# A decoder block on one core: three small edits to its vector work, and a planner that chooses its order with margins and jitter

## The chip, the cores and the metric

One Trainium2 chip, one of its cores. Five engines take part, each with an instruction queue of its own: TensorE (PE: matrix products), VectorE (DVE), ScalarE (ACT), GpSimd (POOL) and SyncE (SP, which issues most of the transfers). The metric is the device time of one execution in microseconds (us), as the median of several runs; less is better.

## The reference

A decoder block on x of 1024 positions by 1024 channels, all in float32. Two mixers share the input projection, a dense gated feed-forward network (FFN) follows, and a final norm:

```python
cond = silu(c) @ ada_w + ada_b                 # shift1, scale1, gate1, shift2, scale2, gate2
h = rmsnorm(x, norm1_g) * (1 + scale1) + shift1
u, v, val, gate = split(h @ w_in + b_in)       # 512 channels each
# mixer A: spatial gating, 8 heads of 64, causal in chunks of 128 positions
v = layernorm(gelu(v), a_ln_g, a_ln_b)
y_a = gelu(u) * (einsum('hts,bcshd->bcthd', tril(w_s), v) + b_s)
# mixer B: gated causal depthwise convolution of width 31, norm by 8 groups, swish
y_b = silu(groupnorm(conv(val * sigmoid(gate)) + conv_b))
x = x + gate1 * (concat(rmsnorm(y_a), rmsnorm(y_b)) @ w_out)
h2 = rmsnorm(x, norm2_g) * (1 + scale2) + shift2
g_ff, up = split(h2 @ w_ffn_in)                # 2 x 2816 channels
x = x + gate2 * ((silu(g_ff) * up) @ w_ffn_out)
out = rmsnorm(x, norm_f_g) * (1 + scale_f) + shift_f
```

## The kernel before

Activations are held transposed, channels on the 128 partitions, and the 1024 positions in two halves of 512; most tiles are 128x512. A float32 product is made of three fp32r products of a high and a low part (`mm3`, L679 to L684, for the mixers; `product`, L1068 to L1074, for the FFN, with `split` at L1064 making the two parts). The FFN uses a seven-product scheme of Strassen's kind, whose PSUM banks appear as A, B and C. `ah` are products of the FFN's first tiles, made ahead while the mixers of the other half still run.

The places that the change touches:

- `v_proj` (L895): the gelu of v leaves PSUM through ScalarE into `vn[half][tch]`, four tiles of 128 positions by 512 channels for each half. Mean and variance go into `mv`, ScalarE takes the root `sd` (L917), DVE its reciprocal (L918), and DVE normalises each tile in place (L921): eight passes of 128x512 in all.
- `spatial` (L941): for each pair of heads, eight small products of 64 columns (L947) fill a PSUM bank `pm` from the four `vn` tiles. One DVE pass scales it and adds the bias into an SBUF tile `mx` (L951), another multiplies `ya`, the gelu of u, by it (L955). Eight of each in all.
- `finish_shift` and `finish_scale` (L646 to L652): DVE adds the bias to a few columns of `cond`, and forms `(1 + scale) * gain`. Each pass is 128 by 8 elements.
- `conv_pair` (L985): the 31 taps of the convolution, most of them on DVE (L1006, `cv`), some as an ACT product and a POOL sum (L1000, L1001).
- `rstd` (L710): sums of squares by narrow products of 32 columns (L727), root on ACT (L730), reciprocal on DVE (L731), spread back by a product of PE (L737).
- the conditioning itself: DVE forms part of the columns of `cond` (L636), POOL and ACT the rest (L633, L634).
- `norm` and `output` (L1370, L1380): the last norm, `rt_nf` on DVE at L1375, spread by PE at L1377, and the output tiles `of` on DVE (L1399), ACT and out by a transfer.

The order on each engine is not that of the code. `fix_order` (L499), called last, has all instructions with their dependences and PSUM slots, gives each a cost, and simulates: `forward` lays them out by rank, `backward` finds for each how long the rest after it takes, and that becomes the next rank. Four such orders are made (a first one and three more), the one that ends first by the simulation is kept, and each engine's row is fixed by dependences that need no semaphore.

Of the kernel before, what the change touches and what calls it, by code (L numbers as in the profile page):

```python
# [67 lines left out]
ENGINES = ("PE", "DVE", "Activation", "Pool", "SP")  # L68
SIGNAL = {"PE": 0.043, "DVE": 0.024, "Activation": 0.024, "Pool": 0.068, "SP": 0.05}
TABLES = ("Sqrt", "Silu", "Sigmoid", "Gelu")  # L70
TABLE_LOAD = 1.295
LOAD_WAIT, STORE_WAIT, LOAD_RATE, STORE_RATE = 2.05, 1.29, 350e3, 376e3
LOAD_GAP, STORE_GAP, TURN_GAP = 0.07, 0.24, 0.3
DMA_ISSUE = 0.44
DMA_AHEAD = 0.5
SHORT_ROWS = 1.15
CLOCK_WINDOW = 3.4133


class Step:  # L80
# [313 lines left out]
def forward(g, rank):  # L394

    import heapq
    count = len(g.steps)
    need, at = [len(s.before) for s in g.steps], [0.0] * count
    done, order = [0.0] * count, {e: [] for e in ENGINES}
    ready, waiting = ({e: [] for e in ENGINES} for _ in range(2))  # L400
    parked = {tag: [] for tag in g.order}
    slots, clock, table = Slots(g), Clock(True), None

    def arrive(n):
        tag, t = slots.blocked_on(g.steps[n])
        if tag is not None:
            parked[tag].append(n)
            return
        heapq.heappush(waiting[g.steps[n].engine], (max(at[n], t), n))

    def wake(tags):
        for tag in tags:
            again, parked[tag] = parked[tag], []
            for n in again:
                arrive(n)

    for s in g.steps:
        if not need[s.n]:
            arrive(s.n)
    for _ in range(count):  # L420
        t, e = pick(clock, ready, waiting)
        while waiting[e] and waiting[e][0][0] <= t + 1e-6:
            n = heapq.heappop(waiting[e])[1]
            heapq.heappush(ready[e], (rank[n], n))
        chosen = ready[e][0]
        if e == "Activation" and g.steps[chosen[1]].table not in (None, table):
            others = [x for x in ready[e] if g.steps[x[1]].table in (None, table)]
            if others and min(others)[0] < chosen[0] + TABLE_LOAD:
                chosen = min(others)
# [12 lines left out]
        for n in s.after:  # L442
            need[n] -= 1
            same = g.steps[n].engine == e and not s.dma
            if (s.n, n) in g.turns:
                at[n] = max(at[n], t + DMA_ISSUE)
            else:
                at[n] = max(at[n], (clock.free[e] if e == "PE" else end) if same else end + SIGNAL[e])
            if not need[n]:
                arrive(n)  # L450
    return order, done, slots.follows
# [44 lines left out]
    return tail  # L496


def fix_order(tc, edges, stacked, reusing, rounds=3):  # L499

    g = Graph(list(tc.nc.cur_bb.bb.instructions), edges, stacked, reusing)
    order, done, follows = forward(g, list(range(len(g.steps))))
    best = max(done), order
    for _ in range(rounds):
        tail = backward(g, [-t for t in done], follows)
        order, done, follows = forward(g, [-t for t in tail])
        best = min(best, (max(done), order), key=lambda b: b[0])
    for steps in best[1].values():
        for earlier, later in zip(steps, steps[1:]):
            tc.add_manual_dep(later.ins, earlier.ins.name,  # L510
                              mybir.DependencyInfo(mybir.DependencyClass.NoSync, mybir.DependencyReason.DATA),
                              reason="fix_order")
# [3 lines left out]
def block_kernel(ctx: ExitStack, tc: tile.TileContext, xT, c, ada, cols, vbias, bs, wsp,  # L516
                 wv, wu, wk, wvg, wo, wf, wfo, wfl, cst, out):
    nc = tc.nc
    V, A, G, PE = nc.vector, nc.scalar, nc.gpsimd, nc.tensor

    edges = []
# [7 lines left out]
    const = ctx.enter_context(tc.tile_pool(name="const", bufs=1))  # L529
# [5 lines left out]
    mid = stage.enter_context(tc.tile_pool(name="mid", bufs=1))  # L535
    front = stage.enter_context(tc.tile_pool(name="front", bufs=1))
# [21 lines left out]
    def tmp(name, dt=F32):  # L558
        return front.tile([P, H], dt, tag="tmp", name=name, bufs=N_TMP)
# [7 lines left out]
    colt = const.tile([P, NCOL], F32, name="colt")  # L567
# [10 lines left out]
    def col(name, i=0):  # L578
        o = _OFF[name] + i
        return colt[:, o:o + 1]  # L580
# [58 lines left out]
    def ccol(m, k, n=1):  # L639
        return cond[:, m * 8 + k:m * 8 + k + n]  # L640

    def bcol(m, k, n=1):
        o = _OFF["ada_b"] + m * 8 + k
        return colt[:, o:o + n]

    def finish_shift(m, k, n):  # L646
        V.tensor_tensor(ccol(m, k, n), ccol(m, k, n), bcol(m, k, n), op=ALU.add)

    def finish_scale(m, gname, k, n):
        o = _OFF[gname] + k  # L650
        V.tensor_tensor(ccol(m, k, n), ccol(m, k, n), bcol(m, k, n), op=ALU.add)
        V.scalar_tensor_tensor(ccol(m, k, n), ccol(m, k, n), 1.0, colt[:, o:o + n],  # L652
                               op0=ALU.add, op1=ALU.mult)


    def weights(src, name, lo_eng, tag="w", parts=1):
# [106 lines left out]
    bst = front.tile([P, 4, P], F32, name="bst")  # L763
# [81 lines left out]
    for k in range(KD):  # L845
        n = len(nc.cur_bb.bb.instructions)
# [13 lines left out]
        t = tmp(f"t_h1_0_{k}")  # L860
# [34 lines left out]
    def v_proj(half, between=None):  # L895
        mv = const.tile([P, 4, 2], F32, name=f"mv{half}")
        sd = const.tile([P, 4], F32, name=f"sd{half}")
        vn[half] = [front.tile([P, H], F32, tag="vn", name=f"vn{half}_{i}", bufs=4) for i in range(4)]
        if not vw:
            vw.extend(weights(wv[i], f"v_{i}", G) for i in range(4))  # L900
        for tch in range(4):
            bank = mm_bank(f"v{half}_{tch}")
            tok = slice(tch * P, (tch + 1) * P)
            for k in range(KD):
                hk = h1[half][k]
                mm3(bank, (hk[:, 0, tok], hk[:, 1, tok]), unit(vw[k // 2], k % 2, 512),
                    k == 0, False)
            PE.matmul(bank, vsel.broadcast_to([P, P]), vb, start=False, stop=True)
            dst = vn[half][tch]
            A.activation(dst, bank, AF.Gelu)  # L910
            st = front.tile([P, 6], F32, tag="bn", name=f"bn{half}_{tch}", bufs=4)
            V.bn_stats(st, dst)
            V.bn_aggr(mv[:, tch, :], st)
            step_background()
            if between is not None and tch == 1:
                between()
        A.activation(sd, mv[:, :, 1], AF.Sqrt, bias=epst[:, 0:1])  # L917
        V.reciprocal(sd, sd)  # L918
        for tch in range(4):
            dst = vn[half][tch]  # L920
            V.tensor_scalar(dst, dst, mv[:, tch, 0:1], sd[:, tch:tch + 1],  # L921
                            op0=ALU.subtract, op1=ALU.mult)

    ya = [None, None]

    def ya_part(half, j):
        return ya[half][j // 2][:, hs(j % 2)]
# [13 lines left out]
    def spatial(half, bank):  # L941
        for hp in range(4):
            pm = bank(f"pm{half}_{hp}")
            for tch in range(4):
                for e in range(2):
                    o = hp * P + e * 64
                    PE.matmul(pm[e * 64:(e + 1) * 64, tch * P:(tch + 1) * P],  # L947
                              vn[half][tch][:, o:o + 64],
                              wt[:, 2 * hp + e, :], start=True, stop=True)
            t = tmp(f"mx{half}_{hp}")  # L950
            V.scalar_tensor_tensor(  # L951
                t.rearrange("p (c t) -> p c t", c=4), pm.rearrange("p (c t) -> p c t", c=4),
                col("a_ln_g", hp), bst[:, hp:hp + 1, :].broadcast_to([P, 4, P]),
                op0=ALU.mult, op1=ALU.add)
            V.tensor_tensor(ya_part(half, hp), ya_part(half, hp), t, op=ALU.mult)  # L955

    def branch_out(half, srcs, gname, name, ssq_groups, add_eng, lo_eng):
        r = rstd(srcs, DA, name, ssq_groups, add_eng)
# [185 lines left out]
    ffn = ctx.enter_context(tc.tile_pool(name="ffn", bufs=1, reuse_waits="tile"))  # L1144
# [44 lines left out]
    for f in range(N_AHEAD, N_AHEAD + N_FILL):  # L1189
        t = ffn.tile([P, 2, H], F32, tag="m3", name=f"ahead_{f}", bufs=4)  # L1190
# [4 lines left out]
    for p in range(4):  # L1195
        b11, b21, b12, b22 = (ev(f"h2_{n}_{p}") for n in ("11", "21", "12", "22"))
        for kh, (t0, t1) in enumerate(((b11, b12), (b21, b22))):
            k = p + 4 * kh
# [59 lines left out]
    order = tile_order()  # L1258
# [236 lines left out]
    output(1)  # L1495
    output(2)

    fix_order(tc, edges, ("mid", "front"), "ffn", 3)


# [79 lines left out]
```

## Time and profile before

| | |
|---|---|
| median of 3 runs | 968.09 us (967.17 to 968.7) |
| the profiled execution's own time | 967.97 us |
| its span in the profile | 965.9 us |
| granted TensorE clock, mean | 0.995 |
| PE, PEld busy | 98%, 80% of the span |
| DVE, ACT, POOL busy | 90%, 49%, 42% |
| moved by transfers | 184 MB, 191 GB/s |

The span runs from the first to the last instruction; 2.07 us of the execution lie around it. PEld is TensorE loading weights, which runs beside its products. A busy PE is not by itself a PE at full rate: matmuls overlap, so the distance between the starts of two matmuls says more than the busy share. A group's row gives the line, the engine and operation, output from inputs, the count, busy us in all and mean ns of one, and then the idle time before and what ended it.

### The profile page before, as it was taken

The numbers are of one execution on the slowest core, as the hardware profiler recorded it, in microseconds if no ns is written. First come the engines' busy times: TensorE is split into PE (matmuls) and PEld (weight loads), VectorE is DVE, ScalarE is ACT, GpSimd is POOL, SyncE is SP. The second block draws the span as 40 slices with busy tenths as digits, with TensorE's granted clock in tenths as the row PEclk, the third lists the DMA queues.
The fourth block names the chain that finished last, engine by engine and source line by source line (L and its number), as shares of the span: only waits on it lengthen the run. The fifth ranks groups of instructions, "written<-read, shape, count | busy, mean of one in ns | idle before, by whom it ended". The sixth has DMA issues, their size and how long they took to land.

```text
span 965.9 us, 12960 instructions
## 1 busy us (share of the span) xinstructions
PE 950.5 (98%) x4521; PEld 769.6 (80%) x4521; DVE 871.7 (90%) x1236; ACT 474.0 (49%) x756; POOL 408.6 (42%) x241
## 2 busy tenths in 40 slices
PE   8999999999999999999999999999999999999996
PEld 4887777778777778788888888888888888888885
DVE  6999999999999763999999999999879999969956
ACT  5787477643474753564333333333337437227426
POOL 0089988836453413665444444455433100000132
PEclk9999999999999999999999999999999999999998
DMA  9882542343485444844677678867657857415104
GB/s 353 323 310 91 176 152 69 113 174 131 137 282 188 158 136 146 271 173 147 215 245 239 230 237 261 268 211 257 211 177 264 266 172 258 162 33 159 61 1 174
DMA packets 70498, 184.24 MB, mean 191 GB/s; under 512 B 7841, under 2 KB 8353, under 8 KB 70434
## 3 DMA queue, kind: packets, MB, share of 16 engines
q1 hardware_dynamic: 70434, 183.43, 56.5%
q8 instruction: 35, 0.57, 0.2%
q14 instruction: 29, 0.24, 0.1%
HBM read 142.24 MB, written 41.16 MB: 190 GB/s over the span
## 4 chain that ended last, share of the span: by engine, by line
PE 79%; DVE 15%; ACT 2%; DMA 2%; issue 1%; SPq 0%; ACTq 0%; DVEq 0%
PE B L1073 30%; PE C L1073 18%; PE ah L1073 10%; DVE cv L1006 5%; PE A L1073 3%; PE v L682 2%; PE v L684 2%; PE po L682 2%; PE po L684 2%; PE v L683 2%; PE po L683 2%; PE p L684 1%; PE p L683 1%; PE p L682 1%; DVE ada L636 1%
## 5 line engine op out<-in xcount | busy, mean ns | idle before, releaser
L1073 PE MATMUL B<-h,w_f 128*128 128x512 f32 x816 | 189.6, 389 | 0.1
L1073 PEld LDWEIGHTS B<-h,w_f 128*128 128x128 f32 x816 | 153.0, 188 | 32.5 <-ACT x L1291 0.8
L1006 DVE SCALAR_TENSOR_TENSOR cv<-ypad,colt,cv 128x512 f32<-128x512 f32 x216 | 147.0, 744 | 0.2
L1073 PE MATMUL B<-fa,w_d 128*128 128x512 f32 x528 | 124.8, 389 | 0.1
L1073 PE MATMUL C<-h,w_f 128*128 128x512 f32 x528 | 123.4, 389 | 0.0
L1073 PEld LDWEIGHTS B<-fa,w_d 128*128 128x128 f32 x528 | 98.8, 188 | 21.4 <-DVE x L1433 0.7
L1073 PEld LDWEIGHTS C<-h,w_f 128*128 128x128 f32 x528 | 99.1, 188 | 20.6
L1073 PE MATMUL ah<-h,wh_a 128*128 128x512 f32 x320 | 102.4, 396 | 0.3 <-ACT h L699 0.3
L1359 POOL TENSOR_TENSOR sq_nf<-sq_nf,sq_nf 128x512 f32<-128x512 f32 (+1 forms) x15 | 18.0, 1202 | 170.2 <-ACT sq_nf L1353 170.0
L666 POOL TENSOR_TENSOR wl_a<-raw_a,wh_a 128x1024 fp32r<-128x1024 f32 x20 | 49.8, 2488 | 78.2 <-ACT wh_a L665 78.2
L1065 ACT ACTIVATE w_d<-raw_d 128x512 fp32r<-128x512 f32 (+1 forms) x72 | 42.0, 593 | 80.9 <-PE B L1073 32.6
L1065 ACT ACTIVATE w_f<-raw_f 128x512 fp32r<-128x512 f32 x68 | 42.5, 629 | 75.9 <-PE B L1073 41.5
L1316 POOL TENSOR_TENSOR x<-x,up 128x512 f32<-128x512 f32 x20 | 33.2, 1659 | 105.6 <-ACT x L1315 105.6
L1066 DVE TENSOR_TENSOR w_f<-raw_f,w_f 128x512 fp32r<-128x512 f32 x68 | 70.2, 1039 | 2.6 <-ACT w_f L1065 2.5
L1073 PEld LDWEIGHTS ah<-h,wh_a 128*128 128x128 f32 x320 | 60.0, 188 | 15.7 <-ACT h L699 1.4
L1073 PE MATMUL C<-fa,w_d 128*128 128x512 f32 (+1 forms) x291 | 63.9, 370 | 0.0
L1073 PE MATMUL ah<-h,wl_a 128*128 128x512 f32 x160 | 62.5, 390 | 0.0
L1073 PEld LDWEIGHTS C<-fa,w_d 128*128 128x128 f32 x291 | 51.0, 188 | 9.2
L1066 DVE TENSOR_TENSOR fa<-a,fa 128x512 fp32r<-128x512 f32 x77 | 52.4, 720 | 0.4 <-ACT fa L1065 0.4
L1433 DVE SCALAR_TENSOR_TENSOR x<-B,cond,x 128x512 f32<-128x512 f32 x48 | 35.6, 745 | 18.2 <-PE B L1073 18.0
L1066 DVE TENSOR_TENSOR w_d<-raw_d,w_d 128x512 fp32r<-128x512 f32 (+1 forms) x72 | 49.1, 691 | 1.1 <-ACT w_d L1065 1.1
L1065 ACT ACTIVATE fa<-a 128x512 fp32r<-128x512 f32 x77 | 46.1, 625 | 7.1 <-DMA a<-acts 4.0
(265 smaller groups left out, 2111.2 us busy)
## 6 DMA issues: line engine op xcount, KB each, us to landing
acts<-x SPq DMA_DIRECT2D x77, 256.0 KB, 2.9
a<-acts SPq DMA_DIRECT2D x77, 256.0 KB, 4.0
raw_f<-wf SPq DMA_DIRECT2D x32, 512.0 KB, 4.0
ada<-ada SPq DMA_DIRECT2D x24, 512.0 KB, 3.5
x<-ada SPq DMA_DIRECT2D x24, 512.0 KB, 4.4
raw_a<-wf SPq DMA_DIRECT2D x20, 512.0 KB, 3.9
ahead<-ahead SPq DMA_DIRECT2D x40, 256.0 KB, 2.6
ypad<-ada SPq DMA_DIRECT2D x16, 512.0 KB, 5.7
```

Of the source, the lines that this page charges most:

```text
L636: V.scalar_tensor_tensor(raw, raw, 1.0, cact, op0=ALU.mult, op1=ALU.mult, accum_out=cond[:, j:j + 1])
L666: lo_eng.tensor_tensor(lo[:, cut], raw[:, cut], hi[:, cut].bitcast(F32), op=ALU.subtract)
L682: PE.matmul(acc, shi, mhi, start=start, stop=False)
L683: PE.matmul(acc, slo, mhi, start=False, stop=False)
L684: PE.matmul(acc, shi, mlo, start=False, stop=stop)
L1006: V.scalar_tensor_tensor(accs[j], src, wc, accs[j], op0=ALU.mult, op1=ALU.add)
L1065: A.activation(dst[:, 0, :], src, AF.Copy)
L1066: lo_eng.tensor_tensor(dst[:, 1, :], src, dst[:, 0, :].bitcast(F32), op=ALU.subtract)
L1073: last_mm = PE.matmul(bank[:, cols], s, m[:, cols], start=first and p == 0 and i == 0, stop=p == n - 1 and i == 2, skip_group_check=True)
L1316: G.tensor_tensor(g0, g0, up0, op=ALU.mult)
L1359: G.tensor_tensor(run, run, t, op=ALU.add)
L1433: V.scalar_tensor_tensor(x_tile(k, part), bank[:, cols], ccol(GATE2, k), x_tile(k, part), op0=ALU.mult, op1=ALU.add)
```

## The change

1. `spatial`: the scaled and biased result is written back to the PSUM bank `pm`, and the product with `ya` reads it there. The SBUF tile `mx` is gone.
2. `v_proj`: a DVE pass of 128x4 forms `nb = -mean * sd`; the eight normalisations become ScalarE activations with `sd` as scale and `nb` as bias.
3. `finish_shift`, `finish_scale`: from DVE to GpSimd; the scale takes three passes in place of two, through a tile `gained`.
4. `fix_order`: the costs of all instructions but PE's are stretched by 1, 1.5 or 2%, those of transfers by 5, 7.5 or 10%. For each of the three margins four ranked orders are made, and of the twelve the one is kept whose mean end is earliest over four replays with random lengthening.

```diff
-def fix_order(tc, edges, stacked, reusing, rounds=3):
+MARGINS = ((1.01, 1.05), (1.015, 1.075), (1.02, 1.1))
+JITTER = (0.008, 0.08)
+TRIALS = 4
+def replay(g, order):
+    ... # runs a given order through the same slots, clock and costs; returns when the last step ends
+@contextmanager
+def stretched(g, factor):
+    kept = [(s, s.issue, s.finish, s.port, s.dma and s.bytes) for s in g.steps if s.engine != "PE"]
+    for s, issue, finish, port, size in kept:
+        f = factor(s)
+        if s.dma:
+            s.bytes = size * f
+        else:
+            s.issue, s.finish, s.port = issue * f, finish * f, port * f
+    yield
...
+def jittered(g, order, seed):
+    rng = random.Random(seed)
+    with stretched(g, lambda s: 1 + abs(rng.gauss(0, JITTER[s.dma]))):
+        return replay(g, order)
+
+def fix_order(tc, edges, stacked, reusing, rounds=4):
     g = Graph(list(tc.nc.cur_bb.bb.instructions), edges, stacked, reusing)
-    order, done, follows = forward(g, list(range(len(g.steps))))
-    best = max(done), order
-    for _ in range(rounds):
-        tail = backward(g, [-t for t in done], follows)
-        order, done, follows = forward(g, [-t for t in tail])
-        best = min(best, (max(done), order), key=lambda b: b[0])
-    for steps in best[1].values():
+    orders = []
+    for margin in MARGINS:
+        with stretched(g, lambda s: margin[s.dma]):
+            order, done, follows = forward(g, list(range(len(g.steps))))
+            for _ in range(rounds):
+                tail = backward(g, [-t for t in done], follows)
+                order, done, follows = forward(g, [-t for t in tail])
+                orders.append(order)
+    times = [sum(jittered(g, order, seed) for seed in range(TRIALS)) for order in orders]
+    best = orders[times.index(min(times))]
+    for steps in best.values():
...
     def finish_shift(m, k, n):
-        V.tensor_tensor(ccol(m, k, n), ccol(m, k, n), bcol(m, k, n), op=ALU.add)
+        G.tensor_tensor(ccol(m, k, n), ccol(m, k, n), bcol(m, k, n), op=ALU.add)
     def finish_scale(m, gname, k, n):
         o = _OFF[gname] + k
-        V.tensor_tensor(ccol(m, k, n), ccol(m, k, n), bcol(m, k, n), op=ALU.add)
-        V.scalar_tensor_tensor(ccol(m, k, n), ccol(m, k, n), 1.0, colt[:, o:o + n],
-                               op0=ALU.add, op1=ALU.mult)
+        G.tensor_tensor(ccol(m, k, n), ccol(m, k, n), bcol(m, k, n), op=ALU.add)
+        gained = const.tile([P, n], F32, name=f"gained{m}")
+        G.tensor_tensor(gained, ccol(m, k, n), colt[:, o:o + n], op=ALU.mult)
+        G.tensor_tensor(ccol(m, k, n), gained, colt[:, o:o + n], op=ALU.add)
...
         V.reciprocal(sd, sd)
+        nb = const.tile([P, 4], F32, name=f"nb{half}")
+        V.scalar_tensor_tensor(nb, mv[:, :, 0], -1.0, sd, op0=ALU.mult, op1=ALU.mult)
         for tch in range(4):
             dst = vn[half][tch]
-            V.tensor_scalar(dst, dst, mv[:, tch, 0:1], sd[:, tch:tch + 1],
-                            op0=ALU.subtract, op1=ALU.mult)
+            A.activation(dst, dst, AF.Identity, bias=nb[:, tch:tch + 1], scale=sd[:, tch:tch + 1])
...
-            t = tmp(f"mx{half}_{hp}")
-            V.scalar_tensor_tensor(
-                t.rearrange("p (c t) -> p c t", c=4), pm.rearrange("p (c t) -> p c t", c=4),
-                col("a_ln_g", hp), bst[:, hp:hp + 1, :].broadcast_to([P, 4, P]),
-                op0=ALU.mult, op1=ALU.add)
-            V.tensor_tensor(ya_part(half, hp), ya_part(half, hp), t, op=ALU.mult)
+            chunks = pm.rearrange("p (c t) -> p c t", c=4)
+            V.scalar_tensor_tensor(chunks, chunks, col("a_ln_g", hp), bst[:, hp:hp + 1, :].broadcast_to([P, 4, P]),
+                                   op0=ALU.mult, op1=ALU.add)
+            V.tensor_tensor(ya_part(half, hp), ya_part(half, hp), pm, op=ALU.mult)
...
-    fix_order(tc, edges, ("mid", "front"), "ffn", 3)
+    fix_order(tc, edges, ("mid", "front"), "ffn")
```

The new planner gives every engine a new row. Lines of the changed kernel stand 66 or 67 further down (L947 becomes L1015, L1006 becomes L1072, L731 becomes L798, L1399 becomes L1465).

On TensorE, at the first products of the spatial mixer for half 0 (`pm0_0` is written `pm_0_1271`; `v` are the wide products of the projection of v for half 1). In the row before:

```order
L683 MATMUL v_1_1359<-wh_v_991,h_1_6_828 128x512
L947 MATMUL pm_0_1271<-wt,vn_0_958 64x128 x2
L947 MATMUL pm_0_1271<-wt,vn_1_959 64x128 x2
L947 MATMUL pm_0_1271<-wt,vn_2_960 64x128 x2
L947 MATMUL pm_0_1271<-wt,vn_3_961 64x128 x2
L947 MATMUL pm_1_1283<-wt,vn_0_958 64x128 x2
```

and in the row now:

```order
L749 MATMUL v_0_1323<-wh_v_991,h_1_6_828 128x512
L1015 MATMUL pm_0_1273<-wt,vn_0_958 64x128 x2
L750 MATMUL v_0_1323<-wh_v_991,h_1_6_828 128x512
L1015 MATMUL pm_0_1273<-wt,vn_1_959 64x128 x2
L751 MATMUL v_0_1323<-wl_v_992,h_1_6_828 128x512
L1015 MATMUL pm_0_1273<-wt,vn_2_960 64x128 x2
L1015 MATMUL pm_1_1284<-wt,vn_0_958 64x128
L1015 MATMUL pm_0_1273<-wt,vn_3_961 64x128 x2
```

They stand in the projection's first chunk (`v_0`) where they stood in its second (`v_1`), that is 26 wide products earlier, and single wide products now lie between them. In the whole row of TensorE the unbroken blocks of narrow products (32 or 64 columns) go from 24 to 28, counted without the very first block, which handles c; one of the four additional ones lies in the head, ahead of the first wide products. The two sums `gn` over the convolution's outputs in half 1 (L1026, `s` by `cstt`), of which there are two pairs, had six and three other products between the two of a pair; now the two stand next to each other, the first of the first pair eight rows later than before.

On VectorE, ahead of the reciprocal for the norm of the second half of x (`rt_n1_1`), taps of the convolution are `cv`, conditioning columns `ada`. In the row before:

```order
73 L636 TENSOR_SCALAR ada20_966,cond_107<-ada20_966,cact_99 128x1024
74 L1006 TENSOR_SCALAR cv0_0_1144<-ypad0_108,colt_74,cv0_0_1144 128x512
75 L1006 TENSOR_SCALAR cv0_1_1145<-ypad1_109,colt_74,cv0_1_1145 128x512
76 L1006 TENSOR_SCALAR cv0_0_1144<-ypad0_108,colt_74,cv0_0_1144 128x512
77 L1006 TENSOR_SCALAR cv0_1_1145<-ypad1_109,colt_74,cv0_1_1145 128x512
78 L731 RECIPROCAL rt_n1_1_783<-rt_n1_1_783 128x128
```

and in the row now:

```order
72 L702 TENSOR_SCALAR ada20_966,cond_107<-ada20_966,cact_99 128x1024
73 L1072 TENSOR_SCALAR cv0_1_1147<-ypad1_109,colt_74,cv0_1_1147 128x512
74 L798 RECIPROCAL rt_n1_1_783<-rt_n1_1_783 128x128
75 L1072 TENSOR_SCALAR cv0_0_1146<-ypad0_108,colt_74,cv0_0_1146 128x512
76 L1072 TENSOR_SCALAR cv0_1_1147<-ypad1_109,colt_74,cv0_1_1147 128x512
```

The reciprocal stands four instructions nearer to the front, one tap behind the same conditioning pass where four stood.

On VectorE at the end of the program (`of1` and `of2` are output tiles of the last two quarters of the positions, `rt_nf2` the last quarter's root). In the row before:

```order
1135 L1399 TENSOR_SCALAR of1_4_8307<-x1_2_81,cond_107,ssq_nf1_8199 128x256 x2
1136 L1375 RECIPROCAL rt_nf2_8290<-rt_nf2_8290 128x2
1137 L1399 TENSOR_SCALAR of1_6_8313<-x1_3_82,cond_107,ssq_nf1_8199 128x256 x2
1138 L1399 TENSOR_SCALAR of2_0_8319<-x1_0_79,cond_107,ssq_nf2_8200 128x256 x2
```

and in the row now:

```order
1111 L1465 TENSOR_SCALAR of1_4_8307<-x1_2_81,cond_107,ssq_nf1_8199 128x256 x2
1112 L1465 TENSOR_SCALAR of1_6_8313<-x1_3_82,cond_107,ssq_nf1_8199 128x256
1113 L1441 RECIPROCAL rt_nf2_8290<-rt_nf2_8290 128x2
1114 L1465 TENSOR_SCALAR of1_6_8313<-x1_3_82,cond_107,ssq_nf1_8199 128x256
1115 L1465 TENSOR_SCALAR of2_0_8319<-x1_0_79,cond_107,ssq_nf2_8200 128x256 x2
```

The last reciprocal stands one pass of 128x256 later.

More of the change, by code (lines that the diff above doesn't have):

```diff
@@ L496, in backward @@
     return tail
-def fix_order(tc, edges, stacked, reusing, rounds=3):
-    g = Graph(list(tc.nc.cur_bb.bb.instructions), edges, stacked, reusing)
-    order, done, follows = forward(g, list(range(len(g.steps))))
-    best = max(done), order
-    for _ in range(rounds):
-        tail = backward(g, [-t for t in done], follows)
-        order, done, follows = forward(g, [-t for t in tail])
-        best = min(best, (max(done), order), key=lambda b: b[0])
-    for steps in best[1].values():
+def replay(g, order):
+    place, done, at = dict.fromkeys(ENGINES, 0), {}, [0.0] * len(g.steps)
+    need = [len(s.before) for s in g.steps]
+    slots, clock, table = Slots(g), Clock(True), None
+    for _ in range(len(g.steps)):
+        best = None
+        for e in ENGINES:
+            if place[e] == len(order[e]) or need[order[e][place[e]].n]:
+                continue
+            s = order[e][place[e]]
+            tag, t = slots.blocked_on(s)
+            t = max(t, at[s.n], clock.free[e])
+            if tag is None and (best is None or t < best[0]):
+                best = t, s
+        t, s = best
+        slots.take(s)
+        if s.table not in (None, table):
+            table, t = s.table, t + TABLE_LOAD
+        begin, end = clock.run(s, t)
+        done[s.n] = end
+        if slots.release(s, end + SIGNAL[s.engine]):
+            slots.hand_over()
+        for n in s.after:
+            need[n] -= 1
+            if (s.n, n) in g.turns:
+                at[n] = max(at[n], t + DMA_ISSUE)
+            elif g.steps[n].engine == s.engine and not s.dma:
+                at[n] = max(at[n], clock.free["PE"] if s.engine == "PE" else end)
+            else:
+                at[n] = max(at[n], end + SIGNAL[s.engine])
+        place[s.engine] += 1
+    return max(done.values())
@@ new lines, in stretched @@
+@contextmanager
[5 more added lines that the diff above has]
+            s.bytes = size * f
+        else:
+            s.issue, s.finish, s.port = issue * f, finish * f, port * f
+    yield
+    for s, s.issue, s.finish, s.port, size in kept:
+        if s.dma:
+            s.bytes = size
+def jittered(g, order, seed):
+    import random
+    rng = random.Random(seed)
+    with stretched(g, lambda s: 1 + abs(rng.gauss(0, JITTER[s.dma]))):
+        return replay(g, order)
```

## The prediction

> **What bounds the kernel now.** I read the page first: the busy shares and the chain that ended last.
>
> ```profile
> PE 950.5 (98%) x4521; PEld 769.6 (80%) x4521; DVE 871.7 (90%) x1236; ACT 474.0 (49%) x756; POOL 408.6 (42%) x241
> ...
> PE 79%; DVE 15%; ACT 2%; DMA 2%; issue 1%; SPq 0%; ACTq 0%; DVEq 0%
> ```
>
> TensorE is busy 98% and carries 79% of the chain, but VectorE has 90%. So I looked at the stages, in the windows of equal length (columns: stretch, length, busy us of PE, PEld, DVE, ACT and POOL with counts, then PE clock, DMA share, GB/s).
>
> ```profile
> 160.00:180.00 20.00, 20.00 (x149) 15.11 (x149) 19.54 (x28) 14.05 (x21) 15.55 (x8) 1.00 0.50 158
> 460.00:480.00 20.00, 20.00 (x90) 16.57 (x89) 19.79 (x25) 6.55 (x11) 8.86 (x6) 1.00 0.62 210
> ```
>
> In both, VectorE is nearly full (19.54 and 19.79 of 20 us), and PE doesn't wait: 20.00 of 20. VectorE runs full beside it, with buffers between. VectorE time removed is worth something only where PE waits for it. Those places are in the list of waits, engine PE (us in all, times, longest).
>
> ```profile
> PE ssq_nf L1377 <- DVE rt_nf L1375: 1.5, 1, 1.5
> ...
> PE ssq_n L737 <- DVE rt_n L731: 1.0, 1, 1.0
> PE ssq_n L825 <- ACT sq_n L823: 0.5, 1, 0.5
> PE ah L1073 <- ACT h L699: 0.3, 1, 0.3
> PE gn L1026 <- DVE s L1049: 0.2, 1, 0.2
> ```
>
> L825 is in the head, as others left out here are, which hang on the first transfers and have none of the edited steps. L1377 is the tail. What remains of note between is 1.0, 0.3 and 0.2 us. So the kernel is bound by TensorE, and there is little to win: the three mid-program waits show 1.5 us idle. A wait costs more than its idle time, as the next matmul starts late too; doubled, 3.0 us is my bound for them.
>
> **The edits on VectorE (1, 2 and 3).** Their prices, from the groups by shape:
>
> ```profile
> L921 DVE TENSOR_SCALAR vn<-vn,mv,sd 128x512 f32<-128x512 f32 x8 | 10.7, 1373 | 0.0
> L955 DVE TENSOR_TENSOR ya<-ya,mx 128x512 f32<-128x512 f32 x8 | 9.6, 1222 | 0.0
> L1318 DVE TENSOR_TENSOR u<-C,u 128x512 f32<-128x512 f32 x22 | 15.0, 682 | 2.2 <-PE C L1073 2.2
> L647 DVE TENSOR_TENSOR cond<-cond,colt 128x8 f32<-128x8 f32 x4 | 3.7, 954 | 0.0
> ```
>
> L921 goes: 10.7 us. L955 gets one input from PSUM; the same operation with a PSUM input is L1318 at 682 ns, so 8 x (1222 - 682) = 4.3 us goes. L951 reads PSUM now and will also write there, a form not in this trace; the two rows with and without a PSUM operand differ by 0.54 us, so between 4.3 less and 4.3 more for its eight; I take no change, as its operand in PSUM stays. The bias passes of L647 go with 3.7 us for four. Two passes `nb` of 128x4 come; the nearest row is the reciprocal of the same shape, below at 0.17 us, so 0.3. In all 10.7 + 4.3 + 3.7 - 0.3 = 18.4 us of VectorE time, 15 of them between 140 and 200 us.
>
> Most of the 1373 and 954 ns isn't work: the one source's own range shows how the same shape takes 541 ns or 2620.
>
> ```profile
> L921 DVE TENSOR_SCALAR vn<-vn,mv,sd x8: 541/1512/2620, 141.3 to 176.8; 128x512 f32<-128x512 f32 x8
> ```
>
> The Trainium skill, SBUF — State Buffer, "Who interferes with whom", speaks of one port pair that VectorE and GpSimd share as an exclusive lock, taken by a `tensor_scalar` in its two-port mode and by passes with two SBUF inputs. The spread in the row agrees. By that rule edit 3 puts ten more GpSimd passes on the same pair, which speaks against it, but the sum would not change while PE doesn't wait for VectorE.
>
> ScalarE and GpSimd pay:
>
> ```profile
> L997 ACT ACTIVATE s<-ypad,colt 128x512 f32<-128x512 f32 x4 | 3.1, 805 | 0.0
> L730 ACT ACT_TABLE_LOAD x5 | 6.4, 1283 | 0.1
> L752 POOL MEMSET ypad<- 128x30 f32 x4 | 0.3, 123 | 0.3 <-POOLq L1568 0.3
> ```
>
> L997 has a scale and a bias column, as the new passes do: 8 x 0.8 = 6.4 us of ScalarE. The new row of ScalarE has two table loads more: 2.6 us. ScalarE is 49% busy. The ten GpSimd passes of 128x8 cost at least 0.123 us each (the small memset), at most the 0.95 of the VectorE row they replace: 1.2 to 9.5 us on an engine that is 42% busy; I take 3. The final ones stand hundreds of us ahead of the FFN's output that reads them. I price all of this at nothing: PE's own queue covers it. If that cover is gone, at the products of `pm`, it is the slower rival below.
>
> **The planner (4): waits.** The largest mid-program wait is at L737. PE, ScalarE and VectorE on their timelines:
>
> ```profile
> 75.81 0.39 PE L683 MATMUL pu<-h,wl_u 128*128 128x512 f32 x1
> ...
> 76.26 0.39 PE L682 MATMUL pu<-h,wh_u 128*128 128x512 f32 x1
> 77.61 1.16 PE L737 MATMUL ssq_n<-rt_n,sel_tok 128*128 128x128 f32 x8 [0.96 <-DVE rt_n L731]
> ...
> 73.83 0.37 ACT L730 ACTIVATE rt_n<-ssq_n,epst 128x128 f32<-128x128 f32 x1
> ...
> 73.98 2.72 DVE L1006 SCALAR_TENSOR_TENSOR cv<-ypad,colt,cv 128x512 f32<-128x512 f32 x4
> 76.61 0.94 DVE L731 RECIPROCAL rt_n<-rt_n 128x128 f32<-128x128 f32 x1
> ```
>
> The root is there at 74.20, but four taps of the convolution stand ahead of the reciprocal, which starts at 76.61. In the new row one tap stands there: three taps less at 2.72 / 4 = 0.68 us is 2.0 us earlier, more than the wait. What it costs now: 77.61 - 76.26, less one interval between wide matmuls, which undisturbed neighbours show: (76.26 - 75.81) / 2 = 0.225. So 1.35 - 0.23 = 1.1 us. It goes. Next on that path is ScalarE's root at 74.20 plus 0.94, and that is early enough. At the sums `gn` of half 1:
>
> ```profile
> 321.49 0.39 PE L1073 MATMUL ah<-h,wh_a 128*128 128x512 f32 x1
> 322.08 1.13 PE L1026 MATMUL gn<-s,cstt 128*128 128x512 f32 x2 [0.20 <-DVE s L1049]
> ...
> 323.51 0.40 PE L1073 MATMUL ah<-h,wh_a 128*128 128x512 f32 x1
> 323.98 1.10 PE L1026 MATMUL gn<-s,cstt 128*128 128x512 f32 x2
> ```
>
> Here 0.59 - 0.23 and 0.47 - 0.23 make 0.6 us; the row records two products at L1026 as one group. With the first of a pair later and the pair together, I take that as gone. The wait for `h` at `ah` (0.3 in the list) I take as gone too: bounds 0 and 0.6. Together 1.1 + 0.6 + 0.3 = 2.0 us.
>
> **The planner: switches.** Each unbroken block of narrow products breaks the even row of wide ones. Two blocks, of 8 and of 24:
>
> ```profile
> 341.93 0.39 PE L684 MATMUL po<-y_a,wh_o 128*128 128x512 f32 x1
> 342.24 0.42 PE L727 MATMUL ssq_b<-sq_b,ones 128*32 128x128 f32 x8
> ...
> 342.93 0.39 PE L683 MATMUL po<-y_a,wl_o 128*128 128x512 f32 x1
> ...
> 384.40 0.39 PE L684 MATMUL po<-y_b,wh_o 128*128 128x512 f32 x1
> 384.72 0.86 PE L727 MATMUL ssq_n<-sq_n,ones 128*32 128x128 f32 x24
> ...
> 385.85 0.39 PE L1073 MATMUL ah<-h,wl_a 128*128 128x512 f32 x1
> ```
>
> From the wide matmul before to the second one after: 1.00 and 1.45 us, where two intervals would be 0.45. So 8 cost 0.55 and 24 cost 1.00; sixteen more cost 0.45, eight 0.22, and 0.33 is left for the block itself. The new row has four blocks more; one is in the head, which waits anyway. Three times 0.33 is 1.0 us; at most, by the whole price of the shorter block, 3 x 0.55 = 1.65; at least nothing, if single narrow products slip in. I take 1.0, for it is measured on the same kinds of product. The Trainium skill, TensorEngine Tiling (Array Packing), "Key Properties", says that changing the tiling mode drains TensorE. The 0.33 us agrees, and by that rule the interleaving is a loss here of the same 1.0.
>
> **The tail.** The last steps, on the timelines:
>
> ```profile
> 957.33 0.16 DVE L1375 RECIPROCAL rt_nf<-rt_nf 128x2 f32<-128x2 f32 x1
> 957.40 0.85 DVE L1399 SCALAR_TENSOR_TENSOR of<-x,cond,ssq_nf 128x256 f32<-128x256 f32 x2
> 957.54 1.23 PE L1377 MATMUL ssq_nf<-eye,rt_nf 128*128 128x128 f32 x4 [1.49 <-DVE rt_nf L1375]
> 958.88 3.22 DVE L1399 SCALAR_TENSOR_TENSOR of<-x,cond,ssq_nf 128x256 f32<-128x256 f32 x8 [0.62 <-PE ssq_nf L1377]
> ```
>
> The reciprocal at 957.33 releases PE, PE the last eight `of` passes, and they the end. In the new row it stands behind one of the two passes of 957.40: 0.85 / 2 = 0.4 us later, and so is everything after it. It can't be more; less only if the pass was done by then.
>
> **Sum.** The profiled execution took 967.97 us, its span 965.9 with 2.1 around it; it is 0.12 under the median of the runs, 968.09, so the sum can be set against either. 967.97 - 2.0 (waits) + 1.0 (switches) + 0.4 (tail) = 967.4.
>
> **The rivals.**
>
> *All waits go (faster).* Costs stretched by a margin make the planner put producers earlier everywhere, and VectorE has 18 us more room. For it: each of the three waits has its producer on VectorE or behind it. Against it: the head and tail can't move by this. The 3.0 us of the bound go, the blocks cost nothing, the tail 0.4: 967.97 - 3.0 + 0.4 = 965.4. With some 0.8 of the head's L825 and its ramp as well, 964.6.
>
> *A late handoff (slower).* The products of `pm` come 26 wide products, 26 x 0.225 = 5.9 us, earlier in half 0, and what feeds them is on another engine:
>
> ```profile
> 139.59 1.04 ACT L634 ACTIVATE ada<-ada 128x1024 f32<-128x1024 f32 x1
> 140.61 0.17 DVE L918 RECIPROCAL sd<-sd 128x4 f32<-128x4 f32 x1
> 147.17 1.97 PE L947 MATMUL pm<-wt,vn 128*64 128x128 f32 x32
> ```
>
> 147.17 - 5.9 is 141.3. The reciprocal ends at 140.78, `nb` at 140.95, and ScalarE's first normalised tile would be there at 140.95 + 0.8 = 141.75 at the pace of this trace. VectorE's relief must win back about half a us, or PE waits, and all wide products behind it in the row with it. If ScalarE is held by one more conditioning sum (1.04), PE waits 1.5 us; each bank is also held by VectorE until its second pass, one L955 of 1.22 longer than now, and the next `pm` waits for it. 1.5 + 1.2 in half 0; half 1 has about one pass more room, so half of that, 1.3. Together 4.0, from 967.4 to 971.4; half 0 alone 970.1. It decides from the point at which `vn0_0` is ready after the PE reaches it.
>
> *Nothing shows (no change).* If VectorE's relief is all hidden, and new waits as large as the removed ones come elsewhere in the new rows: 968.0.
>
> **How the numbers follow.** A measurement of this kernel can tell about 0.2% from no change, 1.9 us: faster is under 966.2, slower over 970.0. The forecast, 967.4, gets 0.30, nothing shows 0.08: same 0.38. All waits gone, 965.4: 0.37, as each of the three waits ends with work of VectorE or behind it, where 18 us of room arise. The late handoff: 0.25, for its half us of missing room. The range starts at 964.6 and ends at 970.6: it holds the forecast, the case without change and the faster case with its bound, and of the late handoff the part in which half 0 alone is late; some 0.05 lies below and 0.12 above.
>
> **What would show it.** Right: no wait at the spreading product of `rt_n1_1` (L804 or near it), VectorE's busy time some 18 us less with PE's waits nearly as before, the windows of 20 us in the FFN still at 20.00 for PE, and the last `rt_nf` one pass later. Wrong on the handoff: PE waits with ScalarE's `vn` (L990) or VectorE's `ya` (L1021) as releasers at 140 to 190 us. Wrong altogether: the distance between wide matmuls is no longer 0.225, or a stretch of PE after 400 us shows idle time.

## The result, and the profile after

The changed kernel took 974.96 us in the median of 13 runs, the kernel before 967.70 in 13: a ratio of 1.0068, 95% interval 1.0054 to 1.0081. The forecast was 967.4 us, with a range up to 970.6 and "the same" as the likeliest outcome; it was wrong: the time lies above the range. The 13 times are not one cluster: eleven lie from 974.04 to 976.02 us with a mean TensorE clock of 0.991 to 0.994, two at 967.75 and 968.17 with 0.996 and 0.995. The profiled execution, 974.04 us with a span of 972.3, is of the larger cluster.

Its page, busy shares and the chain that ended last:

```profile
PE 952.0 (98%) x4521; PEld 771.4 (79%) x4521; DVE 858.6 (88%) x1222; ACT 481.1 (49%) x766; POOL 410.4 (42%) x251
...
PE 88%; DVE 9%; DMA 1%; ACT 1%; issue 1%; POOL 1%; POOLq 0%; ACTq 0%; SPq 0%; DVEq 0%
```

Nothing here looks worse: VectorE has 13 us less, and the chain is more TensorE than it was. The list of waits, engine PE, shows it:

```profile
PE v L749 <- DVE bst L861: 3.9, 1, 3.9
...
PE ssq_nf L1443 <- DVE rt_nf L1441: 1.9, 1, 1.9
...
PE gn L1112 <- DVE sd L985: 1.1, 1, 1.1
PE p L751 <- DVE h L935: 1.0, 1, 1.0
```

The waits at the spreading product (L737 before), at `gn` of half 1 and at `ah` are gone. A wait of 3.9 us is new, at a place that no part of the change names: a product of the v projection whose PSUM bank still holds the sums `rs`, until VectorE has used them for the bias `bst` (L861). The windows ahead of, at and behind it, and two that answer to those of before:

```profile
114.00:118.60 4.60, 0.73 (x5) 0.29 (x3) 4.52 (x10) 1.63 (x3) 0.03 (x1) 1.00 0.54 183
118.60:122.80 4.20, 4.20 (x12) 3.31 (x13) 4.17 (x7) 1.15 (x2) 3.96 (x2) 0.59 0.76 300
160.00:180.00 20.00, 20.00 (x120) 14.67 (x120) 15.01 (x26) 17.25 (x27) 18.11 (x10) 1.00 0.31 106
460.00:480.00 20.00, 20.00 (x89) 16.55 (x89) 20.00 (x24) 5.92 (x10) 10.65 (x7) 1.00 0.46 160
```

At 160 us VectorE fell from 19.54 to 15.01 and ScalarE rose, as the edits want, with TensorE full in both. The loss is in the first two rows: TensorE works 0.73 us of 4.60, and in the stretch behind it the granted clock is 0.59. The timelines of VectorE, GpSimd and TensorE there:

```profile
106.38 8.73 DVE L702 SCALAR_TENSOR_TENSOR ada<-ada,cact 128x1024 f32<-128x1024 f32 x1
117.02 1.44 DVE L861 SCALAR_TENSOR_TENSOR bst<-rs,colt,bst 64x128 f32<-64x128 f32 x4
...
105.66 1.32 POOL L1067 TENSOR_TENSOR s<-s,cp 128x512 f32<-128x512 f32 x1
106.91 2.41 POOL L699 TENSOR_TENSOR ada<-ada,cact 128x1024 f32<-128x1024 f32 x1
109.24 2.43 POOL L733 TENSOR_TENSOR wl_v<-raw_v,wh_v 128x1024 fp32r<-128x1024 f32 x1
111.61 2.42 POOL L699 TENSOR_TENSOR ada<-ada,cact 128x1024 f32<-128x1024 f32 x1
118.84 2.39 POOL L699 TENSOR_TENSOR ada<-ada,cact 128x1024 f32<-128x1024 f32 x1 [4.82 <-DMA ada<-ada]
...
114.33 0.40 PE L975 MATMUL v<-vb,vsel 128*128 128x512 f32 x1
118.60 0.47 PE L749 MATMUL v<-wh_v,h 128*128 128x512 f32 x1 [3.87 <-DVE bst L861]
...
122.78 0.39 PE L751 MATMUL v<-wl_v,h 128*128 128x512 f32 x1
```

One VectorE pass, the conditioning column `ada23`, takes 8.73 us; the shortest pass of this shape takes 1.2, the median of the twelve on `ada` tiles 2.05, and in the trace before the longest of the twelve took 3.34. It starts while GpSimd runs, three more GpSimd passes follow without a gap, and it ends at 115.11, 1.1 us after the last of them, while GpSimd waits for a transfer. The bias sums behind it come at 117.02, and TensorE, which started its last product at 114.33, goes on at 118.60. Then eleven intervals between starts take 122.78 - 118.60 = 4.18 us, where eleven of 0.227 would take 2.50: 1.7 us for the lower clock.

### The profile page after: what moved, and what is told of

Same layout as the page of the kernel before. It is cut to its first block, busy times and chain, and to the rows that moved or that the text cites. A ratio compares the mean times of both kernels' runs of the same rounds, so it can differ in the third digit from the quotient of the medians.

```text
span 972.3 us, 12968 instructions
## 1 busy us (share of the span) xinstructions
PE 952.0 (98%) x4521; PEld 771.4 (79%) x4521; DVE 858.6 (88%) x1222; ACT 481.1 (49%) x766; POOL 410.4 (42%) x251
## 4 chain that ended last, share of the span: by engine, by line
PE 88%; DVE 9%; DMA 1%; ACT 1%; issue 1%; POOL 1%; POOLq 0%; ACTq 0%; SPq 0%; DVEq 0%
PE B L1139 31%; PE C L1139 18%; PE ah L1139 10%; DVE cv L1072 4%; PE A L1139 3%; PE po L749 3%; PE po L751 3%; PE po L750 3%; PE p L751 3%; PE p L749 3%; PE p L750 3%; DVE ada L702 1%; PE pm L1015 1%; PE v L749 1%; PE v L751 1%
## 5 line engine op out<-in xcount | busy, mean ns | idle before, releaser
L1072 DVE SCALAR_TENSOR_TENSOR cv<-ypad,colt,cv 128x512 f32<-128x512 f32 x216 | 148.7, 746 | 0.7
L1132 DVE TENSOR_TENSOR w_f<-raw_f,w_f 128x512 fp32r<-128x512 f32 x68 | 73.8, 1092 | 7.0 <-ACT w_f L1131 7.0
```

What stands on the lines that cost most here:

```text
L1072: V.scalar_tensor_tensor(accs[j], src, wc, accs[j], op0=ALU.mult, op1=ALU.add)
L1132: lo_eng.tensor_tensor(dst[:, 1, :], src, dst[:, 0, :].bitcast(F32), op=ALU.subtract)
```

## The experiments

Theory A: this one hold is the whole loss. VectorE's pass with two SBUF inputs gets no turn while GpSimd's passes follow each other; what stands behind it in VectorE's row makes TensorE wait, and the wait costs clock as well. Theory B: the edits cost (ScalarE's norm late, PSUM banks held longer). Theory C: the new order is worse in many small places.

**The edits without the new planner.** The operations are those of the changed kernel, `fix_order` is that of before (set against the changed kernel, and shortened to the call):

```diff
-    fix_order(tc, edges, ("mid", "front"), "ffn")      # margins, twelve orders, replays
+    fix_order(tc, edges, ("mid", "front"), "ffn", 3)   # the function of before
```

> Edits 1 to 3 with the planner of before. Theory A (one VectorE pass with two SBUF inputs, the conditioning column ada23, is held by an unbroken row of GpSimd passes; the bias sums bst behind it come late, TensorE waits 3.9 us for their bank and then runs 3.5 us at a lower clock): the edits cost nothing by themselves, 966 to 969 us, unless this order too puts that pass beside an unbroken row of GpSimd; then a wait of TensorE at the same place shows it. Theory B (the edits cost: ScalarE's norm is late for pm, or the banks are held longer): 972 to 975 us, with waits at pm. Theory C (the new order is worse in many small places, switches and waits): 967 to 968 us, as the old planner is back.

967.32 us in 11 runs, ratio 1.0003 (0.9994 to 1.0011). Theory B falls: in this order the edits cost nothing, and bring nothing. The same pass on VectorE and its neighbours on GpSimd:

```profile
105.75 2.84 DVE L636 SCALAR_TENSOR_TENSOR ada<-ada,cact 128x1024 f32<-128x1024 f32 x1
...
105.12 2.39 POOL L667 TENSOR_TENSOR wl_v<-raw_v,wh_v 128x1024 fp32r<-128x1024 f32 x1
107.47 3.35 POOL L633 TENSOR_TENSOR ada<-ada,cact 128x1024 f32<-128x1024 f32 x1
```

Here the pass waits for one GpSimd pass, gets its turn at 107.5, and now GpSimd's next takes 3.35 in place of 2.4: whoever is second waits.

**The new planner without the edits.** The operations of before, the new `fix_order`.

> The operations of before in an order by the new planner with margins and jitter. Theory A: what decides is whether a VectorE pass with two SBUF inputs stands beside an unbroken row of GpSimd with TensorE's bank behind it: 966 to 969 us if not, 972 to 975 us with the wait at the bias sums if so. Theory B (the edits cost): 966 to 968 us. Theory C (the new order is worse in many small places): 972 to 975 us without one large wait.

970.67 us in 5 runs, ratio 1.0037 (1.0025 to 1.0049): slower than before, without a wait at the bias sums, and outside the ranges of all three theories. Its waits are many small ones; those listed come to 12.0 us, against 7.9 in the kernel before. Some of the new ones:

```profile
PE pu L748 <- ACT h L765: 1.3, 1, 1.3
PE p L750 <- DVE h L934: 1.2, 1, 1.2
PE po L748 <- ACT y_b L1030: 0.7, 1, 0.7
```

So for these operations the loss is of the kind that theory C names, at a smaller price than it gave. The planner by itself is no gain here; that its order does no such harm with the edits in is seen further down, where the hold is gone.

**The pass moved behind the bias sums.** The changed kernel; in VectorE's row `ada23` goes four places back.

```diff
     best = orders[times.index(min(times))]
+    row = best["DVE"]
+    step = row.pop(find("DVE", "ada23"))
+    row.insert(<behind the first four bst>, step)
```

> The changed kernel; in VectorE's row alone the conditioning pass ada23 is moved four places, from ahead of three taps to behind the first four bias sums bst. Theory A: the pass is still held (from about 109.7 to 115 us, 4 to 6 us long), but the bias sums end at about 109.5 us, TensorE's wait of 3.9 us goes and with it the stretch at a lower clock (1.7 us): 967.5 to 969 us, 5 to 6.5 us less than the changed kernel, and no second cluster of times. Theories B and C: one place in one row changes nothing else, 973 to 975 us.

972.51 us in 6 runs (971.07 to 978.41), ratio 1.0062 (1.0043 to 1.0081). The step that theory A expected happened, and its time didn't come; by the time alone B and C are nearer. On VectorE and GpSimd, in the list of waits, and in a window:

```profile
108.62 1.43 DVE L873 SCALAR_TENSOR_TENSOR bst<-rs,colt,bst 64x128 f32<-64x128 f32 x4
110.08 5.26 DVE L714 SCALAR_TENSOR_TENSOR ada<-ada,cact 128x1024 f32<-128x1024 f32 x1
...
109.48 2.42 POOL L745 TENSOR_TENSOR wl_v<-raw_v,wh_v 128x1024 fp32r<-128x1024 f32 x1
111.83 15.26 POOL L711 TENSOR_TENSOR ada<-ada,cact 128x1024 f32<-128x1024 f32 x6
...
PE gn L1124 <- DVE sd L997: 2.8, 1, 2.8
...
144.00:146.00 2.00, 2.00 (x15) 1.18 (x11) 1.93 (x4) 2.00 (x4) 0.00 (x0) 0.50 0.00 0
```

The bias sums are early, the wait of 3.9 us is gone, the pass is still held, for 5.26. But the time that VectorE lost is missing at the next point where TensorE needs it, the reciprocals for `gn` at 142 us: 2.8 us of wait instead of 1.1, and half the clock behind it (0.50 from 144 to 146 us). So the hold does make the wait at the bias sums, as theory A says; its price I got wrong: the hold itself must go, for what it delays is moved along the row and not saved.

**A gap in GpSimd's row.** The changed kernel; two neighbours of GpSimd's row change places, so that it waits for ScalarE once.

```diff
+    row = best["Pool"]
+    at = find("Pool", "wl_v", find("Pool", "ada"))
+    row[at - 1], row[at] = row[at], row[at - 1]
```

> The changed kernel; in GpSimd's row alone two neighbours are exchanged: the low part wl_v_992 ahead of the conditioning product ada_1028. GpSimd then has to wait about 1.2 us for ScalarE's wh_v at about 107 to 108 us, a gap in its unbroken row. Theory A: the VectorE pass ada23 gets in at the gap, takes 1.2 to 3 us in place of 8.7, TensorE's wait and the lower clock go: 967 to 968.5 us, though GpSimd was made to wait. Rival D (the pass waits for its own transfer, not for GpSimd): it ends at 115 us as before, 973 to 975 us.

967.34 us in 11 runs (966.80 to 968.90), ratio 0.9999 (0.9991 to 1.0008), as theory A had it. VectorE and GpSimd:

```profile
107.07 1.67 DVE L711 SCALAR_TENSOR_TENSOR ada<-ada,cact 128x1024 f32<-128x1024 f32 x1
...
106.36 1.29 POOL L1076 TENSOR_TENSOR s<-s,cp 128x512 f32<-128x512 f32 x1
108.87 2.39 POOL L742 TENSOR_TENSOR wl_v<-raw_v,wh_v 128x1024 fp32r<-128x1024 f32 x1 [1.21 <-ACT wh_v L741]
```

Making GpSimd idle for 1.21 us makes the kernel 6.7 us faster (0.9999 against 1.0068, of 967 us). The pass takes 1.67, no large wait of TensorE is left in the middle, and none of the 11 runs is in the upper cluster. The rival that the pass waits for its own transfer falls with it, since its transfer wasn't touched.

**The changed kernel twice more, each with a profile.**

> The changed kernel once more, with a profile. Theory A: ada23 on VectorE takes 7 to 9 us with TensorE's wait (974 to 976 us), or, in one run of six or so, gets its turn early, with no wait and TensorE's clock at 1.00 around 120 us (967.5 to 968.5 us). No other stage differs between the two.

> The same as the run before: either cluster, told apart by the length of ada23's pass on VectorE alone.

976.03 and 967.14 us: one of each cluster. First the one with the hold, then the one without, VectorE's pass and GpSimd's passes:

```profile
108.40 8.71 DVE L702 SCALAR_TENSOR_TENSOR ada<-ada,cact 128x1024 f32<-128x1024 f32 x1
...
107.67 1.32 POOL L1067 TENSOR_TENSOR s<-s,cp 128x512 f32<-128x512 f32 x1
108.92 2.39 POOL L699 TENSOR_TENSOR ada<-ada,cact 128x1024 f32<-128x1024 f32 x1
111.25 2.42 POOL L733 TENSOR_TENSOR wl_v<-raw_v,wh_v 128x1024 fp32r<-128x1024 f32 x1
113.61 2.42 POOL L699 TENSOR_TENSOR ada<-ada,cact 128x1024 f32<-128x1024 f32 x1
```

```profile
106.86 1.65 DVE L702 SCALAR_TENSOR_TENSOR ada<-ada,cact 128x1024 f32<-128x1024 f32 x1
110.41 1.44 DVE L861 SCALAR_TENSOR_TENSOR bst<-rs,colt,bst 64x128 f32<-64x128 f32 x4
...
106.11 1.32 POOL L1067 TENSOR_TENSOR s<-s,cp 128x512 f32<-128x512 f32 x1
107.36 3.39 POOL L699 TENSOR_TENSOR ada<-ada,cact 128x1024 f32<-128x1024 f32 x1
...
115.03 0.39 PE L749 MATMUL v<-wh_v,h 128*128 128x512 f32 x1
114.00:118.60 4.60, 4.60 (x22) 3.80 (x21) 4.49 (x9) 2.35 (x4) 4.60 (x3) 1.00 0.66 203
```

The same instructions in the same order: in both the pass starts 0.7 us into the same GpSimd pass. Without the hold it is served when that pass ends, and GpSimd's next takes 3.39. With it GpSimd goes first three times running. Without it the bias sums are done at 111.85, 3.2 us ahead of TensorE at 115.03; the hold takes 7.1 us (8.73 - 1.65), so 3.9 of it reach TensorE. In both executions with the hold VectorE was served only when GpSimd's next pass had to wait for a transfer, 4.82 and 5.02 us. What decides the turn where both are ready remains open.

**The hold tried in the kernel before.** Nothing of the change; in VectorE's row `ada23` goes back by four taps, and in a second kernel by seven places.

```diff
+    row = best[1]["DVE"]
+    at = find("DVE", "ada23")
+    row.insert(at + 4, row.pop(at))     # second kernel: at + 7
```

> The kernel before, edits and planner as they were; in VectorE's row alone the conditioning pass ada23 is moved four convolution taps later, so that it starts at about 106.9 us instead of 104.2. There GpSimd has begun its products (106.4 us) and has six passes of 2.4 us in a row. Theory A (a VectorE pass with two SBUF inputs gets no turn while GpSimd passes follow each other without a gap): the pass is held for 5 to 14 us, the bias sums behind it come 3 to 12 us later than at 112.5 us, and TensorE waits at the second chunk of v and then runs at half clock for some us: 972 to 985 us, possibly two clusters of times. Theories B (edits) and C (new planner) have nothing to say here, since neither is in it: 966.5 to 968 us, within 0.2% of before.

> As the last try on the kernel before, but the conditioning pass ada23 stands seven places later in VectorE's row, behind the two sums s, so that it should start at about 108 us, inside GpSimd's unbroken row (from 106.2 us on); in the last run it started 0.03 us after GpSimd's pass and took 1.2 us, GpSimd 3.5. Theory A: held for at least 2 us and for 5 to 14 us if GpSimd's passes follow without a gap; the bias sums come behind it, TensorE waits at the second chunk of v for what the hold exceeds about 5 us, with half the clock after a wait of over 2.5 us: 968 to 982 us. Without a hold at GpSimd: 966.5 to 968 us.

967.39 us in 12 runs, ratio 1.0009 (0.9998 to 1.0019), and 966.48 in 11, ratio 0.9992 (0.9980 to 1.0004). Neither is in the upper cluster, and both miss what theory A expected with a hold (972 to 985 and 968 to 982); one run of each stands out, at 971.07 and 970.61. VectorE and GpSimd of the first, and of the second:

```profile
106.22 1.21 DVE L645 SCALAR_TENSOR_TENSOR ada<-ada,cact 128x1024 f32<-128x1024 f32 x1
...
106.19 3.48 POOL L642 TENSOR_TENSOR ada<-ada,cact 128x1024 f32<-128x1024 f32 x1 [1.05 <-DMA ada<-ada]
```

```profile
107.48 1.42 DVE L645 SCALAR_TENSOR_TENSOR ada<-ada,cact 128x1024 f32<-128x1024 f32 x1
...
105.42 2.40 POOL L642 TENSOR_TENSOR ada<-ada,cact 128x1024 f32<-128x1024 f32 x1 [0.84 <-DMA ada<-ada]
107.77 3.41 POOL L675 TENSOR_TENSOR wl_v<-raw_v,wh_v 128x1024 fp32r<-128x1024 f32 x1
```

In the first VectorE started with GpSimd and GpSimd was held. In the second it waited 0.3 us and got the next turn. So theory A is too strong as it was put: standing beside an unbroken GpSimd row isn't enough for a hold. I could not bring the hold about at will, only take it away. (The 2.5 us in the second expectation is a choice between the waits of 1.1 us, with no lower clock behind it, and of 2.8; no run shows where the limit lies.)

**Better versions tried.** The first is the swapped kernel with TensorE's wait in the head and the tail mended, the second the kernel before with its two largest waits mended; both by moves in the rows alone.

```diff
+    row = best["DVE"]                              # first: h1_0_1 one place nearer to the front,
+    row.insert(find("DVE", "of1_4"), <rt_nf2>)     # both: the last reciprocal ahead of of1_4,
+    row = best["Activation"]
+    row.insert(find("Activation", "of1_2"), <rt_nf2>)   # its root ahead of of1_2
+    row = best["DVE"]
+    row.insert(at - 3, <rt_n1_1>)                  # second: this reciprocal three places earlier
```

> The changed kernel with the exchange on GpSimd of the run before, and two more moves: on VectorE the second tile of h in the head goes ahead of the conditioning pass that stands before it, and the last root rt_nf2 goes two output passes nearer to the front on ScalarE and VectorE. TensorE's wait of 1.0 us in the head should fall to about 0.3 as before (0.65 less), the tail should end 0.9 us earlier: 967.3 - 1.5 = 965.8 us, a ratio of 0.9985 to before. If head and tail are hidden by something else, 967.3.

> The kernel before with two moves in its order and nothing of the change: the reciprocal rt_n1_1 three places nearer to the front on VectorE (TensorE's wait of 1.0 us at the spreading product should go: 1.1 us), and the last root rt_nf2 two output passes nearer to the front on ScalarE and VectorE (0.5 to 0.9 us at the tail). Theory: TensorE's few waits are the whole of what order can win here: 967.0 - 1.8 = 965.2 us, ratio 0.998.

966.93 us in 11 runs, ratio 0.9995 (0.9987 to 1.0004), and 967.52 in 11, ratio 0.9994 (0.9985 to 1.0003): neither can be told from the kernel before, and the 965.8 and 965.2 expected were not reached. In the lists of waits, first of the one, then of the other:

```profile
PE ssq_nf L1460 <- DVE rt_nf L1458: 0.7, 1, 0.7
PE p L768 <- DVE h L952: 0.6, 1, 0.6
```

```profile
PE ssq_nf L1391 <- DVE rt_nf L1389: 0.7, 1, 0.7
...
PE pu L696 <- ACT h L713: 0.4, 1, 0.4
```

The tail's wait fell from 1.9 and 1.5 to 0.7, as meant. The others came back further on (0.6 at a later tile of the head, 0.4 at `pu`). No version here beats the kernel before.

## Why the prediction was wrong

- **The step that failed** is the one that priced VectorE's and GpSimd's new rows at nothing: "the sum would not change while PE doesn't wait for VectorE". The planner's new order got terms for three waits, for switches and for the tail, and none for VectorE passes that come to stand beside GpSimd's. I had read TensorE's cover as if it were without bound, because the profile showed no wait. It is bounded at each handoff by how early the producer is; at the bias sums that is 3.2 us, and a hold of 7.1 us exceeds it. The spread that I quoted for L921, 541 to 2620 ns, was the warning: passes of VectorE already took nearly five times their shortest. I took their mean as a price and never asked what the longest one stands ahead of. The size could not be read off, though: the longest `ada` pass before took 3.34 us. And no sign that I named for being wrong pointed at the bias sums.
- **The rule that I cited spoke against the change, and I set it aside.** The Trainium skill, SBUF — State Buffer, "Who interferes with whom", says that the shared port pair is an exclusive lock and that the other fully blocks. The runs agree that one engine blocks the other: GpSimd's pass takes 3.35 to 3.48 us in place of 2.4 when VectorE is served ahead of it. The 8.73 us on VectorE's side are more than the one GpSimd pass in front of it, and there the measurement decides. But the passes that I charged with it, the ten small ones of edit 3, were not the ones (with the old planner they cost nothing); it was the new place of old ones.
- **The late-handoff rival** had the right kind, a late producer ahead of TensorE, at a smaller price (4.0 us; the hold cost 6.9) and in the wrong place. At `pm` ScalarE's tiles are in time: in the swapped kernel the weight loads for `pm` wait 0.5 us in all for ScalarE's `vn`, and the products of `pm` don't appear in the list of waits. The waits were at the bias sums and, behind them, 1.1 us at `gn` with VectorE late.
- **The rest of the sum fits, in part by luck.** The execution without the hold, which differs by the hold and what follows from it, took 967.14 us, the swapped kernel 967.34, for 967.4 forecast. But the kernel before took 967.70, and so small a difference can't be told from none. The wait at the spreading product is gone and the tail's wait went from 1.5 to 1.9, the forecast 0.4. Whether the first was worth its 1.1 us is not shown: in the second kernel of the hold tried, whose rows are those of before up to there, that wait is missing too, and the second of the better versions, without it and with 0.8 less at the tail, took 967.52 us where the kernel before took 967.59 on the same occasion. VectorE's busy time is 19.5 us less in the execution without the hold (871.7 to 852.2 by the pages), for 18.4 forecast; that too is partly chance, as four passes of `finish_scale` (1.5 us) that I didn't count are gone as well, and the twelve `ada` passes take 25.3 us where they took 21.6. In the changed kernel's groups:

```profile
L990 ACT ACTIVATE vn<-vn,nb,sd 128x512 f32<-128x512 f32 x8 | 5.9, 802 | 1.1 <-DVE nb L987 1.0
L1019 DVE SCALAR_TENSOR_TENSOR pm<-pm,colt,bst 128x512 f32<-128x512 f32 x8 | 5.8, 749 | 2.5 <-PE pm L1015 2.5
L1021 DVE TENSOR_TENSOR ya<-ya,pm 128x512 f32<-128x512 f32 x8 | 5.2, 676 | 0.0
```

ScalarE's pass costs 802 ns (805 taken), VectorE's product 676 (682 taken), and writing back to PSUM changes L951's 738 ns to 749: nothing. What I missed is a wait of 1.0 us in the head, where the new row puts a conditioning pass ahead of a tile of `h`; I had written that "the head and tail can't move by this". I priced the added blocks of narrow products at 1.0 us. Between 100 and 240 us, where three of the four lie, the intervals between one wide product and the next exceed 0.227 us by 21.5 us in all before, and by 22.8 in the execution without the hold: 1.3 more. Waits lie in both, and not quite the same products, so the blocks were not measured apart.
- **The loss adds up.** The execution with the hold took 974.04 us, the one without 967.14: 6.9 us. TensorE's row is the same in both, so the starts can be set against each other one by one. The first falls 4.0 us behind at the bias sums, 1.7 in the stretch at the lower clock and 1.2 at `gn`: 6.9. Before the hold it was 0.5 ahead, and at the tail it loses 0.4, which nearly cancel. In the second execution with the hold the same three places cost 4.0, 1.7 and 1.2; its other 1.5 us are lost in the head.

## What to carry to other kernels

A profile without a wait says that every handoff was in time, not by how much: before an order is changed, look for the longest single passes of the engine that runs beside the bound one, and at what stands right behind them in its row. Where two engines share ports, a pass can wait longer than for the one pass in front of it, so a plan that lets each have its turn in order of arrival (as this planner's `Clock.run` does: `t = max(t, self.port)`, then `self.port = t + s.port`) was too hopeful here, in a row that it had packed without a gap. And when times fall into two clusters, profile one of each before anything else.

## What the runs showed of the hardware

- A waiting VectorE pass isn't always next: three GpSimd passes in a row went ahead of it, for 8.73 and 8.71 us, in two of three profiled executions of one program, and in the third it was served at the first change. A wait of 1.21 us put into GpSimd's row took the hold away in 11 of 11 runs.
- A TensorE wait of 2.8 us was followed by half the clock (0.50 in the third experiment), one of 3.9 us by a stretch at 0.59 that cost 1.7 us more; the waits of 1.7 us in the head and of 1.1 us at `gn` were followed by a clock of 1.00. The Trainium skill, TensorE: Matmul & The Clock Gate, "What's actually happening", gives an idle window of about 3.4 us; the wait of 2.8 us here is shorter than that.
